# Experts by 64 places, two side by side on TensorE, with unsplit float32 weights

## The chip, the cores and the metric

The kernel runs on 1 core of one Trainium2 chip. The metric is the device time of one execution in microseconds. Three runs of the kernel before took 2030.39, 2038.42 and 2041.88 us; the median is 2038.42 us.

## The reference

Two transformer blocks over 256 tokens of width 1024. The first block is a mixer (Hyena, Fourier and mLSTM branches, merged by gates) and a mixture of experts; the second has four layers of attention and feed-forward. The change is in the mixture of experts, which ends the first block:

```python
g_logits = (t @ moe_rg_w + moe_rg_b)                     # 4 groups, top 1
e_logits = (t @ moe_re_w + moe_re_b).reshape(256, 4, 4)  # 4 experts in each, top 2 of the group chosen
combine  = sum(one_hot(e_idx, 16) * w_sel)               # 256 x 16, two entries a token
hg, hu = t @ moe_w_gate[e], t @ moe_w_up[e]              # 1024 x 256 each, 16 experts
a = silu(hg) * hu * combine
out = sum_e a @ moe_w_down[e]                            # 256 x 1024
x = x + mod_l[5] * out;  then rmsnorm(x, norm_f_w)
```

Every token goes to one group and to two of its four experts. With the inputs that the reference draws, the groups get 58, 53, 86 and 59 tokens, and the fullest expert 53. The weights of one expert are 3 MB of float32, those of all sixteen 50.3 MB.

## The kernel before

Nearly all products are made in three fp32r matmuls: each operand is split into a high and a low part (`split` and `unit`: a copy on ScalarE, line 240, and a subtraction on VectorE, line 242), and `mm3_steps` (lines 254 to 256) multiplies high by high, high by low and low by high. Weights arrive on SyncE's queue in pieces of 512 KB in a ring of `raw` tiles (4 of 4 KB in each partition). Memory is taken by hand from two arenas, one of float32 and one of fp32r words. The order of the instructions on each engine comes from a planner that goes by simulated times, except where `c.after(...)` fixes it; a branch (`tc.If`) is a border that nothing is moved across.

In `moe` the logits are made, then `route` picks group and experts in some forty small VectorE operations. `places` counts by matmuls, for each token, how many of its group come earlier, and loads the largest group's size into a register. `experts` works by groups: a group has 128 places, `oh` holds a 128 x 128 matrix of marks for each half of the tokens and each group, and `gather` (line 1382) multiplies the normed tokens by the marks, which brings the tokens of two groups into their places, already transposed; ScalarE and VectorE scale, shift and split them (lines 1384 to 1386). Then the 16 experts run one after the other over the 128 places of their group. Each has four pieces of gate and up weights (two 256 KB loads, rows of 1 KB, 24 matmuls of 512 columns), SiLU and product (lines 1431, 1433), two transposes (1444) and two pieces of down weights (rows of 4 KB, 12 matmuls of 512 columns). After the fourth expert of a group its sum goes back to the tokens by 8 matmuls with the transposed marks (1417). Five more `raw` tiles and two more pairs serve this stage.

At the end `add_experts` multiplies the sums by the modulation row and adds them to `xs` (lines 1502, 1503). Then a branch (line 1493) would do all experts once more for places 128 and up; it is not taken here. The second block begins in `enter`: VectorE weights the tokens (line 2037), TensorE transposes them (370), they are split, and the first projection starts (264, 265). `mod_row` makes a modulation row from float32 matmuls of 32 columns in four column groups of TensorE (line 684); its calls for row 2 run beside the merging of the branches, those for row 5 fill gaps around the logits. PSUM has 5 buffers `acc` (also used for transposes, `tr`) and 3 buffers `mm`.

Of the kernel before, what the change touches and what calls it, by code (L numbers as in the profile page):

```python
# [29 lines left out]
ARENA = {F32: (22528, 1312), F32R: (29696, 1344)}  # L30
RAW, PAIRS, MM, PROBS, AHEAD = 4, 3, 3, 8, 2
# [45 lines left out]
class Arena:  # L77


    def __init__(self, ap, words, kept):  # L80
        self.ap, self.clock, self.kept, self.words = ap, 0, words - kept, words
        self.free = [(0, words - kept, 0)]
        self.rings, self.groups, self.compact = {}, {}, False

    def alloc(self, n):
        n = -(-n // 16) * 16
        best = None
        for i, (at, _, _) in enumerate(self.free):
            end, age = at, 0
            for j in range(i, len(self.free)):  # L90
                a, b, t = self.free[j]
                if a != end:
                    break
# [12 lines left out]
    def keep(self, n):  # L106

        at = self.kept
        self.kept = at + -(-n // 16) * 16
        assert self.kept <= self.words, self.kept  # L110
        return self.ap[:, at : at + n]
# [4 lines left out]
    def ring(self, group, tag, n, bufs):  # L116
# [9 lines left out]
        return self.ap[:, at : at + n]  # L126

    def release(self, pieces):
        self.free += [(a, b, self.clock) for a, b in pieces]
        merged = []  # L130
        for a, b, t in sorted(self.free):
            if merged and merged[-1][1:] == (a, t):
                a = merged.pop()[0]
# [16 lines left out]
class Core:  # L150


    def __init__(self, tc, I, ctx):
# [7 lines left out]
        for dt, (words, kept) in ARENA.items():  # L161
            t = self.const.tile([P, words], dt, name=f"arena{len(self.arenas)}")
            self.arenas[dt] = Arena(t, words, kept)
        self.raw(), self.split_pair()
# [4 lines left out]
        nc.gpsimd.dma_start(self.ident, I["ident"])  # L169

# [14 lines left out]
    def first_block_done(self):  # L185
        for dt, (_, kept) in ARENA.items():
# [273 lines left out]
def host_constants1():  # L460
# [31 lines left out]
    c["slots"] = f32(np.concatenate([before, np.ones((P, P)), np.tile(s[None], (P, 1))], 1))  # L492
# [16 lines left out]
LATER = (0, 2, 4, 6)  # L509
MORE = (5, 2)  # L510
# [3 lines left out]
FILL = (3, 4, 1)  # L514


class Block1:
# [689 lines left out]
    def mod_row(self, m):  # L1207
# [38 lines left out]
    def route_weights(self):  # L1246
# [4 lines left out]
        self.before, self.ones, self.iota = (const[:, i] for i in range(3))  # L1251
        raw = self.tile((KT, 20), F32, "rwr", 1, "rt")
# [31 lines left out]
    def route(self, pss, r):  # L1284
# [7 lines left out]
        gh = self.gh = self.tile((2, 4), F32, "group", 1, "moe")  # L1292
# [5 lines left out]
        def top(src, oh):  # L1298
# [11 lines left out]
        yield  # L1310
        ex, s = tile(2, 4), tile(2)
        v.tensor_tensor(ex, g, along(mx), ALU.subtract)
        nc.scalar.activation(ex, ex, AF.Exp)
# [7 lines left out]
        m2 = top(eg, h2)  # L1321
        q, d = tile(2), tile(2)
# [10 lines left out]
        v.tensor_tensor(self.comb.rearrange("p t (g j) -> p t g j", g=4),  # L1333
                        h1.rearrange("p t (o j) -> p t o j", o=1).to_broadcast([P, 2, 4, 4]), by, ALU.mult)
        yield

    def places(self):

        c, nc = self.c, self.nc
        ps, sums = c.tr(), c.tr()[:, :4]  # L1340
        gh = self.gh
        mm = nc.tensor.matmul
        mm(ps[:, 0:4], self.before, gh[:, 0], start=True, stop=True)
        mm(ps[:, 4:8], self.before, gh[:, 1], start=True, stop=False)
        mm(ps[:, 4:8], self.ones, gh[:, 0], start=False, stop=True)
        self.pos = self.tile((2, 4), F32, "pos", 1, "moe")
        nc.vector.tensor_copy(self.pos, ps[:, :8].rearrange("p (t g) -> p t g", t=2))
        mm(sums, self.ones, gh[:, 0], start=True, stop=False)
        mm(sums, self.ones, gh[:, 1], start=False, stop=True)
# [6 lines left out]
    def experts(self, xp, first, unit):  # L1356
# [4 lines left out]
        parts = lambda shape, tag, bufs=1: self.parts(shape, tag, bufs, "moe")  # L1361
        pos = self.pos
        if first:
            pos = tile((2, 4), F32, "later")
            nc.vector.tensor_scalar(pos, self.pos, float(-first), None, ALU.add)

        oh, ohT = tile((2, 4, P), F32R, "oh"), tile((4, 2, P), F32R, "ohT")
        for q in range(4):
            for t in range(2):
                nc.vector.tensor_scalar(oh[:, t, q], self.iota, pos[:, t, q : q + 1], self.gh[:, t, q : q + 1], ALU.is_equal, ALU.mult)  # L1370

        def gather(p):
# [818 lines left out]
```

## Time and profile before

| | |
|---|---|
| median of 3 runs | 2038.42 us |
| the profiled execution: time, span | 2037.31 us, 2035.5 us |
| PE, PEld, DVE, ACT busy | 95%, 76%, 66%, 51% |
| granted TensorE clock, mean | 0.973 |
| moved by DMA | 364.61 MB, 179 GB/s |

Times are microseconds from the span's start. The 40 slices of the page are 50.9 us each; the expert stage (459 to 620 us) covers slices 11 and 12 of them, counted from 1, where the DMA engines moved 321 and 323 GB/s, the highest of the page. A float32 matmul stands in the trace as two records, one for each pass; fp32r matmuls as one.

### The profile page before, as it was taken

The numbers are of one execution on the slowest core, as the hardware profiler recorded it, in microseconds if no ns is written. First come the engines' busy times: TensorE is split into PE (matmuls) and PEld (weight loads), VectorE is DVE, ScalarE is ACT, GpSimd is POOL, SyncE is SP. The second block draws the span as 40 slices with busy tenths as digits, with TensorE's granted clock in tenths as the row PEclk, the third lists the DMA queues.
The fourth block names the chain that finished last, engine by engine and source line by source line (L and its number), as shares of the span: only waits on it lengthen the run. The fifth ranks groups of instructions, "written<-read, shape, count | busy, mean of one in ns | idle before, by whom it ended". The sixth has DMA issues, their size and how long they took to land.

```text
span 2035.5 us, 27804 instructions
## 1 busy us (share of the span) xinstructions
PE 1931.8 (95%) x10012; PEld 1546.8 (76%) x10012; DVE 1336.6 (66%) x2324; ACT 1035.3 (51%) x1656; POOL 135.9 (7%) x259
## 2 busy tenths in 40 slices
PE   6998998989998999999999999999999999999997
PEld 2886886867786678887888877887767888767886
DVE  4689887868897775556555466556566555867555
ACT  5555654546774744434655555443563444454442
POOL 2110000000002000002111200000110000300000
PEclk8999998989998899999999999999999999989999
DMA  9546644777995356654543456664554655435662
GB/s 310 162 140 194 183 139 147 236 247 245 321 323 162 116 166 199 186 176 131 170 136 110 147 178 202 191 186 145 156 176 129 201 187 176 155 104 175 188 189 80
DMA packets 272403, 364.61 MB, mean 179 GB/s; under 512 B 17018, under 2 KB 206677, under 8 KB 272256
## 3 DMA queue, kind: packets, MB, share of 16 engines
q1 hardware_dynamic: 264832, 338.38, 52.5%
q0 software_dynamic: 7424, 24.36, 3.8%
q8 instruction: 81, 1.33, 0.3%
q14 instruction: 66, 0.54, 0.1%
HBM read 359.53 MB, written 3.15 MB: 178 GB/s over the span
## 4 chain that ended last, share of the span: by engine, by line
PE 59%; DVE 6%; ACT 2%; DMA 1%; issue 1%; POOL 0%; SPq 0%; DVEq 0%; ACTq 0%; POOLq 0%
PE mm L254 14%; PE mm L255 13%; PE mm L256 13%; PE acc L254 4%; PE acc L256 4%; PE acc L255 4%; PE acc L1752 1%; PE acc L1650 1%; DVE arena L242 1%; PE acc L1929 1%; PE acc L2117 1%; ACT arena L240 1%; DVE arena L2014 1%; PE acc L1749 1%; DMA arena<-in_w_gate_up 1%; PE acc L1925 1%
## 5 line engine op out<-in xcount | busy, mean ns | idle before, releaser
L242 DVE TENSOR_TENSOR arena<-arena,arena 128x1024 fp32r<-128x1024 f32 x597 | 716.9, 1213 | 480.6 <-ACT arena L240 475.8
L240 ACT CAST arena<-arena 128x1024 fp32r<-128x1024 f32 x597 | 614.0, 1039 | 549.4 <-PE mm L256 298.9
L254 PE MATMUL mm<-arena 128*128 128x512 f32 (+1 forms) x1856 | 703.3, 385 | 12.7 <-ACT arena L240 6.8
L255 PE MATMUL mm<-arena 128*128 128x512 f32 (+1 forms) x1856 | 706.0, 381 | 0.3 <-DVE arena L242 0.3
L256 PE MATMUL mm<-arena 128*128 128x512 f32 (+1 forms) x1856 | 698.7, 380 | 3.5 <-DVE arena L1386 1.3
L254 PEld LDWEIGHTS mm<-arena 128*128 128x128 f32 x1856 | 352.9, 191 | 85.8 <-ACT arena L240 8.3
L256 PEld LDWEIGHTS mm<-arena 128*128 128x128 f32 x1856 | 352.3, 191 | 71.2 <-DVE arena L219 4.1
L255 PEld LDWEIGHTS mm<-arena 128*128 128x128 f32 x1856 | 354.0, 191 | 61.5 <-issue 1.8
L254 PE MATMUL acc<-arena 128*128 128x512 f32 (+5 forms) x736 | 235.5, 360 | 7.3 <-ACT arena L218 7.3
L255 PE MATMUL acc<-arena 128*128 128x512 f32 (+5 forms) x736 | 235.4, 351 | 0.5 <-DVE arena L219 0.5
L256 PE MATMUL acc<-arena 128*128 128x512 f32 (+4 forms) x736 | 231.8, 350 | 0.0
L218 ACT CAST arena<-acc 128x512 fp32r<-128x512 f32 (+2 forms) x174 | 92.7, 542 | 179.1 <-PE acc L2117 79.8
L219 DVE TENSOR_TENSOR arena<-acc,arena 128x512 fp32r<-128x512 f32 (+2 forms) x174 | 108.1, 632 | 99.1 <-ACT arena L218 98.7
L254 PEld LDWEIGHTS acc<-arena 128*128 128x128 f32 (+1 forms) x736 | 125.0, 190 | 40.3 <-issue 11.6
L255 PEld LDWEIGHTS acc<-arena 128*128 128x128 f32 (+1 forms) x736 | 125.7, 190 | 21.6 <-issue 1.8
L256 PEld LDWEIGHTS acc<-arena 128*128 128x128 f32 (+1 forms) x736 | 124.7, 190 | 20.5 <-DVE arena L219 1.7
L1685 ACT ACTIVATE arena<-arena,nm 128x128 f32<-128x128 f32 (+2 forms) x128 | 65.9, 517 | 27.1 <-DVE nm L1684 27.1
L768 DVE SCALAR_TENSOR_TENSOR arena<-arena 128x192 f32<-128x192 f32 (+1 forms) x160 | 64.9, 430 | 2.4 <-ACT arena L766 0.9
L1684 DVE CUSTOM_DVE_ANT_0 arena<-acc,arena 128x128 f32<-128x128 f32 (+2 forms) x128 | 53.1, 465 | 13.6 <-PE acc L256 13.6
L370 PE MATMUL acc<-arena 128*128 128x128 f32 x200 | 32.9, 302 | 24.1 <-DVE arena L1020 8.2
L370 PEld LDWEIGHTS acc<-arena 128*128 128x128 f32 x200 | 24.4, 153 | 34.8 <-DVE arena L1020 8.3
L2101 ACT ACTIVATE arena<-mm 128x256 f32<-128x256 f32 x88 | 32.4, 379 | 24.4 <-PE mm L256 11.9
(354 smaller groups left out, 1497.8 us busy)
## 6 DMA issues: line engine op xcount, KB each, us to landing
arena<-in_w_gate_up SPq DMA_DIRECT2D x352, 256.0 KB, 4.0
arena<-in_w_down SPq DMA_DIRECT2D x88, 512.0 KB, 3.6
arena<-in_b_w_qkv SPq DMA_DIRECT2D x144, 256.0 KB, 3.0
arena<-in_w_in SPq DMA_DIRECT2D x56, 512.0 KB, 4.0
arena<-in_ada_w SPq DMA_DIRECT2D x48, 512.0 KB, 5.7
arena<-in_moe_w_gate SPq DMA_DIRECT2D x64, 256.0 KB, 4.6
arena<-in_moe_w_up SPq DMA_DIRECT2D x64, 256.0 KB, 4.9
arena<-in_moe_w_down SPq DMA_DIRECT2D x32, 512.0 KB, 5.3
```

What stands on the lines that cost most here:

```text
L218: self.nc.scalar.copy(h, src)
L219: self.nc.vector.tensor_sub(l, src, h.bitcast(F32))
L240: nc.scalar.copy(h[:, : nk * n], raw[:, : nk * n])
L242: nc.vector.tensor_sub(l[:, : nk * n], raw[:, : nk * n], h[:, : nk * n].bitcast(F32))
L254: yield t.matmul(out, x[0], w[0], start=start, stop=False)
L255: yield t.matmul(out, x[0], w[1], start=False, stop=False)
L256: yield t.matmul(out, x[1], w[0], start=False, stop=stop)
L370: self.nc.tensor.transpose(ps[:, j * P : (j + 1) * P], src[:, j * P : (j + 1) * P], self.ident)
L768: nc.vector.scalar_tensor_tensor(ov[:, rows], x, w, ov[:, rows], ALU.mult, ALU.add)
L1684: nc.vector.tensor_tensor_reduce(pr, s, mask, -0.125, 3e38 if sink is None else sink, ALU.add, ALU.min, nm)
L1685: nc.scalar.activation(pr, pr, AF.Exp, bias=nm, scale=-1.0, accum_out=l)
L2101: nc.scalar.activation(s, ps[:, :256], AF.Silu)
```

## The change

- Each expert has 64 places of its own (`SEATS`), so `marks` are by expert (256 x 16), and `places` counts by expert. The marks are made by two VectorE comparisons of 128 x 1024 instead of eight of 128 x 128.
- Two experts run side by side: one writes PSUM partitions 0 to 63, the other 64 to 127, that is, halves of TensorE's columns. Weights and tokens are plain float32 and are not split: no copy on ScalarE and no subtraction on VectorE for them. Gate and up are matmuls of 256 columns, down of 512.
- Gate and up weights are read as `(p k) n`, four rows of a partition at once: 4 KB rows, 512 KB loads. The gather takes every eighth column of the tokens to match, and scale and shift (`A2e`, `S2e`) are brought into that order through DRAM by four small DMAs on GpSimd's queue.
- 9216 words of the fp32r arena are switched to float32 during the experts: nine further pieces (`MORE`) beside the four `raw` tiles. They are taken in turn.
- The sums: `acc` starts from `xs` (four float32 matmuls with the identity), the modulation row is multiplied in before the marks bring the pair's result back, and 8 matmuls do so for every pair. `add_experts` goes; `enter` reads the sums from PSUM.
- The branch for fuller experts (over 64 tokens; three more passes over all experts) comes inside, behind the second pair's transposes. Behind a pair's SiLU and product come, in this order: the 8 matmuls that bring back the pair before, four transposes (the product and the marks), a part of the next gather, down, and another part of the gather. Two small float32 matmuls a pair turn the token weights into weights of places.
- `mod_row` takes its two PSUM tiles from `mm` instead of `acc`, for row 2 too; the filling is 4, 4 instead of 3, 4, 1 steps.

```diff
+MORE, SEATS, YP, AMID = 9, 64, 2, 1
-FILL = (3, 4, 1)
+FILL = (4, 4)
@@ Core @@
+    def close_switched(self):
+        a = self.arenas[F32R]
+        a.free = [f for f in a.free if f[0] < a.words]
+        self.arenas["switched"] = Arena(self.switched_room(F32, "f"), SWITCHED)
@@ mod_row @@
-            ps, out = c.acc()[:, :256], c.acc()
+            ps, out = c.mm()[:, :256], c.mm()
@@ route @@
+        v.tensor_tensor(both, h1, h2, ALU.add)
+        v.tensor_tensor(self.marks.rearrange("p t (g j) -> p t g j", g=4), spread(both), by, ALU.mult)
@@ experts @@
+        def mark():
+            seats = self.iota[:, :SEATS].rearrange("p (o s) -> p o s", o=1).to_broadcast([P, 16, SEATS])
+            for t in range(2):
+                at = pos[:, t].rearrange("p (e o) -> p e o", o=1).to_broadcast([P, 16, SEATS])
+                nc.vector.tensor_tensor(oh[:, t], seats, at, ALU.is_equal)
+        def gather_two(h, g, k):
+            ps = c.mm().rearrange("p (k s) -> p k s", k=2)
+            for j in range(2):
+                cols = slice(k + j, None, KT)
+                for i in range(4):
+                    mm(ps[:, j], xp[i // 2][i % 2][:, cols], marks(i // 2, 4 * g, 4), start=i == 0, stop=i == 3)
+                nc.scalar.activation(h[:, k + j], ps[:, j], AF.Identity, bias=self.S2e[:, k + j], scale=self.A2e[:, k + j])
+        def scatter(p, ohT, y):
+            yp = self.parts((D,), "y", YP, "moe")
+            for n in range(2):
+                sl = slice(512 * n, 512 * n + 512)
+                f = tile((512,), F32, "yf", 2)
+                nc.vector.tensor_tensor(f, y[n], self.rows[5][:, sl], ALU.mult)
+                c.split(*(a[:, sl] for a in yp), f)
+            yield
+            for t in range(2):
+                for n in range(2):
+                    for i in range(2):
+                        mm(acc[t][n], ohT[:, t], yp[i][:, 512 * n : 512 * n + 512], start=False, stop=first == 0 and p == 7 and i == 1)
+            yield
+        for p in range(8):
+            if p % 2 == 0 and p < 6:
+                later = gather(p // 2 + 1)
+            hq = [h[:, :, p % 2 * P + 64 * e : p % 2 * P + 64 * e + 64] for e in range(2)]
+            ps = c.acc()
+            for k in range(0, KT, 4):
+                for i, name in enumerate(("moe_w_gate", "moe_w_up")):
+                    us = [load(I[name][0, 2 * p + e].rearrange("(p k) n -> p k n", p=P)[:, k : k + 4]) for e in range(2)]
+                    for j in range(4):
+                        for e in range(2):
+                            mm(ps[64 * e : 64 * e + 64, 256 * i : 256 * i + 256], hq[e][:, k + j], us[e][:, j], start=i + k + j == 0, stop=i + k + j == KT)
...
+            nc.scalar.activation(s, ps[:, :256], AF.Silu)
+            nc.vector.scalar_tensor_tensor(a, ps[:, 256:], weight[:, p : p + 1], s, ALU.mult, ALU.mult)
+            next(late, None)
...
+            if p == AMID and amid is not None:
+                with self.tc.If(amid > SEATS):
+                    for n in range(SEATS, 256, SEATS):
+                        self.experts(xp, acc, n, raw)
+                    mark()
+                    for k in range(0, KT // 2, 2):
+                        gather_two(following, 1, k)
+            following = next(later, None)
+            y = [c.mm(), c.mm()]
+            for kk in range(2):
+                wd = [load(I["moe_w_down"][0, 2 * p + e, kk * P : (kk + 1) * P].rearrange("p (o n) -> p o n", o=1)) for e in range(2)]
+                for n in range(2):
+                    for e in range(2):
+                        mm(y[n][64 * e : 64 * e + 64], aT[:, kk, 64 * e : 64 * e + 64], wd[e][:, 0, 512 * n : 512 * n + 512], start=kk == 0, stop=kk == 1)
+            late = scatter(p, ohT, y)
+            next(late)
+            following = next(later, None)
@@ moe @@
+        c.close_switched()
+        acc = [[c.acc() for n in range(2)] for t in range(2)]
+        for t in range(2):
+            for n in range(2):
+                with c.after(c.last(PE)):
+                    nc.tensor.matmul(acc[t][n], c.ident, xs[t][:, 512 * n : 512 * n + 512], start=True, stop=False)
-        self.add_experts(self.experts(xp, 0, unit), xs)
-        with self.tc.If(most > P):
-            self.add_experts(self.experts(xp, P, own_unit), xs)
+        self.experts(xp, acc, 0, lambda: next(rooms), most)
@@ enter @@
-                nc.vector.tensor_tensor(zs[t][:, sl], xs[t][:, sl], nf[:, sl], ALU.mult)
+                nc.vector.tensor_tensor(zs[t][:, sl], ps, nf[:, sl], ALU.mult)
```

## Rows read from the trace of the kernel before

**Rows 1.** The page: busy time of the engines, and the chain's shares by engine.
```profile
PE 1931.8 (95%) x10012; PEld 1546.8 (76%) x10012; DVE 1336.6 (66%) x2324; ACT 1035.3 (51%) x1656; POOL 135.9 (7%) x259
PE 59%; DVE 6%; ACT 2%; DMA 1%; issue 1%; POOL 0%; SPq 0%; DVEq 0%; ACTq 0%; POOLq 0%
```

**Rows 2.** Windows: length, busy PE, PEld, DVE, ACT, POOL; clock, DMA share, GB/s.
```profile
459.00:619.60 160.60, 154.10 (x688) 123.16 (x687) 136.46 (x151) 116.86 (x149) 0.00 (x0) 0.99 0.86 288
540.00:600.00 60.00, 60.00 (x268) 48.60 (x268) 54.78 (x58) 46.96 (x59) 0.00 (x0) 1.00 1.02 346
570.00:580.00 10.00, 10.00 (x46) 8.10 (x45) 9.37 (x11) 7.90 (x9) 0.00 (x0) 1.00 1.07 372
619.60:629.10 9.50, 1.82 (x9) 1.60 (x9) 6.78 (x13) 3.52 (x4) 2.10 (x4) 0.62 0.11 33
326.00:374.00 48.00, 47.43 (x280) 37.50 (x279) 39.20 (x59) 19.47 (x30) 3.88 (x8) 1.00 0.66 224
```

**Rows 3.** Groups by line, 459 to 619.6: busy us, mean ns, idle before.
```profile
L242 DVE TENSOR_TENSOR arena<-arena,arena 128x1024 fp32r<-128x1024 f32 x92 | 110.4, 1223 | 17.5 <-ACT arena L240 15.3 <-DMA arena<-in_moe_w_up 0.6 <-DMA arena<-in_moe_w_down 0.3
L254 PE MATMUL mm<-arena 128*128 128x512 f32 x160 | 64.6, 404 | 0.0
```

**Rows 4.** Chain of waits by time, 640 us: start, us, what (start to start).
```profile
640.00 0.24 PE mm L254
640.23 0.23 PE mm L255
```

**Rows 5.** Timeline, end of the stage: start, us, engine, line, tiles, [idle before, releaser].
```profile
617.23 2.36 PE L1417 MATMUL acc<-arena 128*128 128x512 f32 x8
618.93 1.29 DVE L1502 TENSOR_TENSOR arena<-acc,arena 128x512 f32<-128x512 f32 x2 [0.32 <-PE acc L1417]
626.53 2.50 DVE L2037 TENSOR_TENSOR arena<-arena 128x512 f32<-128x512 f32 x4 [2.72 <-DVEq L1493]
627.27 1.97 PE L370 MATMUL acc<-arena 128*128 128x128 f32 x8 [7.68 <-DVE arena L2037]
629.07 0.80 PE L264 MATMUL mm<-arena 128*128 128x512 f32 x1
```

**Rows 6.** Line 1493, the branch: count, ns min/median/max, first to last start.
```profile
L1493 PEldq COMPARE_BRANCH  x1: 3599/3599/3599, 618.7 to 618.7; - x1
L1493 SPq COMPARE_BRANCH  x1: 50/50/50, 614.9 to 614.9; - x1
L1493 SPq EVENT_SEMAPHORE  x8: 17/17/17, 619.2 to 619.7; - x8
```

**Rows 7.** Timeline of PE: float32 in column groups, and what follows.
```profile
428.15 1.50 PE L684 MATMUL acc<-arena 128*32 128x256 f32 x24
429.59 0.33 PE L370 MATMUL acc<-arena 128*128 128x128 f32 x1
...
1080.64 1.09 PE L1929 MATMUL acc<-arena 128*64 128x128 f32 x16
1081.67 0.50 PE L254 MATMUL mm<-arena 128*128 128x512 f32 x1
```

**Rows 8.** Timeline of PE: gather, transposes, small float32 matmuls, first expert.
```profile
529.57 0.63 PE L1382 MATMUL mm<-arena 128*128 128x256 f32 x4
530.03 0.38 PE L1444 MATMUL mm<-arena 128*128 128x128 f32 x2
...
456.95 1.92 PE L1399 MATMUL acc<-arena,arena 128*128 128x4 f32 x16 [0.18 <-DVE arena L1333]
458.73 0.48 PE L254 MATMUL mm<-arena 128*128 128x512 f32 x1
```

**Rows 9.** Lines 1382, 1384 and 1370 alone: ns min/median/max, first to last.
```profile
L1382 PEld LDWEIGHTS mm<-arena x64: 186/188/338, 450.4 to 532.9; 128*128 128x128 f32 x64
L1384 ACT ACTIVATE arena<-mm,arena x16: 557/564/567, 451.8 to 533.4; 128x256 fp32r<-128x256 f32 x16
L1370 DVE TENSOR_SCALAR arena<-arena x8: 337/340/345, 449.3 to 451.3; 128x128 fp32r<-128x128 f32 x8
```

**Rows 10.** Timeline: routing's small operation, and the first gather.
```profile
447.00 0.17 DVE L1305 TENSOR_TENSOR arena<-arena,r 128x8 f32<-128x8 f32 x1
...
450.38 2.27 PE L1382 MATMUL mm<-arena 128*128 128x256 f32 x12 [0.85 <-DVE arena L1370]
```

More of the change, by code (lines that the diff above doesn't have):

```diff
@@ L30 @@
 ARENA = {F32: (22528, 1312), F32R: (29696, 1344)}
+SWITCHED = 9216
 RAW, PAIRS, MM, PROBS, AHEAD = 4, 3, 3, 8, 2
@@ L91, in alloc @@
                 a, b, t = self.free[j]
-                if a != end:
+                if a != end or i < j and a == self.words:
                     break
@@ L1354, in places, with experts @@
         return nc.values_load(most_i[0:1, 0:1], min_val=0, max_val=256)
-    def experts(self, xp, first, unit):
+    def experts(self, xp, acc, first, raw, amid=None):
         c, nc, I = self.c, self.nc, self.I
         tile = lambda shape, dt, tag, bufs=1: self.tile(shape, dt, tag, bufs, "moe")
-        parts = lambda shape, tag, bufs=1: self.parts(shape, tag, bufs, "moe")
+        mm = nc.tensor.matmul
         pos = self.pos
         if first:
-            pos = tile((2, 4), F32, "later")
+            pos = tile((2, 16), F32, "later")
@@ L1389, in marks_T @@
-        def marks_T(q):
-            ps = c.mm()
-            for t in range(2):
-                nc.tensor.transpose(ps[:, t * P : (t + 1) * P], oh[:, t, q].bitcast(F32), c.ident)
-            nc.scalar.copy(ohT[:, q].rearrange("p t s -> p (t s)"), ps[:, : 2 * P])
-        *_, h = gather(0)
-        wp = c.tr()
-        for q in range(4):
-            for t in range(2):
-                nc.tensor.matmul(wp[:, 4 * q : 4 * q + 4], oh[:, t, q].bitcast(F32), self.comb[:, t, 4 * q : 4 * q + 4], start=t == 0, stop=t == 1)
@@ new lines, in experts @@
+        late, later = iter(()), iter(())
+        for p in range(8):
+            if p % 2 == 0 and p:
+                h = following
+            if p % 2 == 0 and p < 6:
[8 more added lines that the diff above has]
+                            mm(ps[64 * e : 64 * e + 64, 256 * i : 256 * i + 256], hq[e][:, k + j], us[e][:, j], start=i + k + j == 0, stop=i + k + j == KT)
+            wp = c.mm()[:, :2]
+            for t in range(2):
+                mm(wp, marks(t, 2 * p, 2).bitcast(F32), self.comb[:, t, 2 * p : 2 * p + 2], start=t == 0, stop=t == 1)
+            for e in range(2):
+                rows = slice(64 * e, 64 * e + 64)
+                nc.scalar.copy(weight[rows, p : p + 1], wp[rows, e : e + 1])
@@ L1451, in moe @@
+            next(late)
+            following = next(later, None)
+        next(late)
     def moe(self, xs, fill):
         c, nc = self.c, self.nc
+        c.close_switched()
         def filler(n):
@@ L1571, in run @@
                 self.dump(f"mix{t}", xs[t])
-            self.moe(xs, self.mod_row(5))
-            for t in range(2):
-                self.dump(f"moe{t}", xs[t])
+            sums = self.moe(xs, self.mod_row(5))
             drop("moe", "mrow5")
-        return xs
+        return xs, sums
 def rope_tables(c):
```

193 lines of the change are left out of this document (86 added, 107 removed).

## The prediction

> **What bounds the kernel now.** The page comes first. TensorE is busy 95% of the span and holds 59% of the chain; VectorE follows with 66% and 6% [rows 1]. So a change pays where it takes TensorE's time away or closes a gap of it, unless the weights then arrive too slowly. The windows of the expert stage come next. From 459.0 to 619.6, 160.6 us, TensorE is busy 154.1 at a clock of 0.99, and the DMA engines move 288 GB/s; from 540 to 600 TensorE has no gap at all, while the DMA share stands at 1.02 and 346 GB/s [rows 2]. Two limits therefore lie close together here, and the change touches both. The groups by line say what TensorE does: 160 matmuls of 512 columns on line 254, as many on 255 and 256, and 32 on each of the three lines for down, 576 in all; VectorE spends 110.4 us on the low parts of weights [rows 3]. In a dense stretch a matmul follows the other every 0.23 us [rows 4], so that 576 make 133 us of the stage's 160.6. Last comes its end in the timeline: the last sum is done at 619.6, VectorE adds it to the tokens, passes the branch, and only at 629.07 does the second block's first projection start [rows 5].
>
> I compare the time between two events that both kernels have: the first expert matmul, at 458.73 [rows 8], and that first projection, at 629.07 [rows 5]: 170.3 us.
>
> **Part by part, TensorE.** Two experts in two halves of the columns, in float32, two passes each. The trace has this form: line 1929, 64 columns wide, 16 records from 1080.64 to the next matmul at 1081.67, 1.03 us. If the halves ran one after the other, these would be 16 steps of 128 columns; line 684 makes six steps of four groups with 256 columns in 1.44 us (428.15 to 429.59) [rows 7]. With x for a step of 128 columns, 2x for 256 and s for entering and leaving the form, 8x + s = 1.03 and 12x + s = 1.44, so x = 0.10 and s = 0.2. Eight steps, not sixteen, fit: the halves do run together. I take 0.215 for 256 columns (bounds 0.205 and 0.24, that is 1.44/6) and 0.43 for 512.
>
> Of a pair: gate and up are 8 slices of the depth by 2 names by 2 passes, 32 steps of 256, 6.9 us; down is 2 by 2 by 2, 8 steps of 512, 3.4 us. Eight pairs make 82.6 us. Bringing the results back is 8 matmuls for every pair instead of every four experts: 64 by 0.231 = 14.8 us. The gathers of groups 1 to 3 stay on this path: 96 matmuls by 0.115 (four from 529.57 to 530.03 [rows 8]) = 11.0. Transposes, four a pair, 32 by 0.12 (0.19 at most, a pair of them 0.38 [rows 8]) = 3.8. The small float32 matmuls are 4 records a pair by 0.11 (16 from 456.95 to 458.73 [rows 8]) = 3.6. Entering and leaving the halves twice a pair by 0.2 = 3.4. Sum 119.2 us, where 154 were busy.
>
> Waits on this path: the first pair has nothing to fill the time of SiLU and product, 1.0; the last two pairs have no gather between transposes and down, 0.8 each; behind the last down three evacuations of some 0.65 (as line 1502 [rows 5]) and their signals, 2.2. Sum 4.8. In the other pairs the 8 matmuls of the pair before (1.86) cover SiLU and product, and a part of the gather (0.9) covers the copies.
>
> The branch. TensorE's own jump took 3.6 us at 618.7, SyncE's 4.2 (614.9 to 619.2) [rows 6]. It now falls between full engines, and what hid it (the end of the stage) is gone: 3.6, and 1.0 more because the clock had fallen to 0.62 in the gap around the old one [rows 2]. Behind SyncE's branch stand all loads from the second pair's down weights on. Before it twenty pieces are issued, so TensorE has work for one and a half pairs, about 20 us, while the queue stands; I cost that at nothing. If the eight waits that followed SyncE's branch [rows 6] now hold it until the loads in flight have landed, up to 8 us.
>
> Its sum: 119.2 + 4.8 + 4.6 = 128.6 us from the first expert matmul to the last sum; before it was 160.9 (458.73 to 617.23 + 2.36).
>
> **The splits** go: 92 subtractions of 1.2 us [rows 3] and as many copies. VectorE is left with about 4 us a pair, ScalarE with 4.5 (two gather activations of 0.56 [rows 9] in each part included); neither is late. What is late next is TensorE itself, and close to it the weights.
>
> **The weights.** 96 pieces of 0.524 MB. Thirteen fit; I take them as there when the first pair starts, as their room comes free when the merging ends. The other 83 are 43.5 MB: at 372 GB/s, the best ten microseconds before [rows 2], 117 us, which with 4 us for the last to land and 6 for what follows it is 127, just inside 128.6. At 346 it is 126 + 10 = 136. Rows of 4 KB alone do not occur in a row of the trace; I take 372 as the value, as the stretch with 346 was bound by TensorE. The Trainium skill (DMA: Bandwidth & Descriptors, Specifications) gives 358 GB/s as one core's share of the memory; the 372 here is above it, and the measurement decides. By the page's figure the estimate would be 121.5 + 10 = 131.5, 3 us more.
>
> **Ahead of the stage.** Counting now needs both choices, about 14 small operations more at 0.2 us each in the chain (0.17 busy [rows 10]), +2.8. Against it VectorE is free of weight splits that stood between these operations, -3; two comparisons of 1.2 us replace eight of 0.34 [rows 9], 0; the four added matmuls with the identity (8 passes of 0.43, 3.4 us) lie beside the routing. The first gather, at 450.38 [rows 10], takes 8 activations of 0.56, 4.5 us. I leave 458.7 as the start, within 5 us on either side.
>
> **Behind the stage.** `add_experts` and the branch go from the chain: instead of 9.5 us from the last sum to the projection [rows 5], I reckon 4.5: one weighting, 0.65, straight from PSUM, two transposes with their splits. Four of five `acc` buffers are still held there, so transposes go one by one: the second half of the tokens pays 3 more later on (0 to 4). And row 2's `mod_row` takes `mm` buffers from the merging in a stretch where TensorE is busy 47.4 of 48 us [rows 2]: 2 (0 to 5).
>
> Sum: 128.6 + 4.5 = 133.1 against 170.3, -37; +5 for the last two; so -32 from the profiled execution's 2037.3 (span 2035.5 and 1.8 around it): 2005. This execution lies 1.1 below the median of the runs, so I call it 2005 to 2006 and give 2005.
>
> **Rivals.**
> - *The weights set the end.* 346 GB/s or less, or SyncE held behind the branch: +8 to +15, 2013 to 2020. For it: DMA share 1.02 already at 346 [rows 2]. Against: 372 was reached with shorter rows.
> - *The gather's strided columns.* Its stationary operand, now every eighth float32, is loaded more slowly than in 188 ns [rows 9]. The slowest load of that line, at the lower clock, took 338 [rows 9]; a step of 0.23 instead of 0.115 for 128 matmuls is +15, 2020. The sign turns where a gather matmul takes 0.25 us more (32/128), a step of 0.37; at 0.48 it is +47, 2052, slower than before. For it: all 128 gather matmuls stand on TensorE's path. Against: nothing in the trace reads with this step, but a load lies beside the matmul before it. The Trainium skill speaks for it (SBUF — State Buffer, Door 1: The DMA port swizzle): memory lines are 16 bytes, and every access to a new line pays; a step of 32 bytes meets a new line each time. No row here shows such a load.
> - *It doesn't do what it says*: an expert with over 64 tokens takes the branch, three more passes of at least 117 us, near 2400. The fullest has 53; next to nothing.
>
> **How the numbers follow.** Forecast 0.62 (its own range 1996 to 2012); weights 0.17; gather at about double 0.12; gather slow enough to be slower than before, with the branch taken, 0.05; nearly no change, by several half-sized losses, 0.04. Runs of this kernel can't tell less than about 0.5% (10 us) from no change. Faster: 0.62 + 0.17 + 0.12 = 0.91, and 0.01 of the fourth case's edge, 0.92; same 0.03; slower 0.05. Range: below, the start 5 us early, no loss at the end and behind (-5) and a dearer merging spared (-2), 1993; above, weights and a doubled gather in part together, 2026.
>
> **What would show it.** After: no line-242 work in the stage; the last sum some 128 us after the first expert matmul; steps of 0.215 with both halves starting together; gather steps of 0.115; at the second pair one gap of about 4 us on TensorE; the DMA near 340 to 375 GB/s. Wrong if TensorE has gaps that end with a landing weight in most pairs, if gather steps are 0.2 and more, if the clock falls in the stage for longer than at the branch, or if the stretch around 326 to 374 grows by more than 5 us.

## The result, and the profile after

The changed kernel is slower. Its median is 2049.2 us (2047.6 to 2056.9, 12 runs) beside 2033.6 us of the kernel before on the same chips (12 runs): a ratio of 1.0073, 95% interval 1.0055 to 1.0090, some 15 us. The forecast was 2005. The profiled execution took 2048.9 us, its span 2047.1. Line numbers below are those of the changed kernel unless another is named.

The page of the changed kernel, its first part and the chain's shares by engine, beside [rows 1]:

```profile
span 2047.1 us, 27688 instructions
PE 1943.5 (95%) x10188; PEld 1515.4 (74%) x10188; DVE 1212.8 (59%) x2192; ACT 948.9 (46%) x1587; POOL 138.6 (7%) x263
PE 65%; DVE 6%; ACT 2%; DMA 1%; issue 1%; POOL 0%; DVEq 0%; SPq 0%; ACTq 0%; POOLq 0%
```

The splits are gone (VectorE 124 us less than before), yet TensorE is busy 12 us longer. Where the time went is seen by comparing events that both kernels have. The first token transposes for the logits start at 418.3 instead of 409.0: 9.3 us are lost before the experts begin. The first expert matmul stands at 469.6 (before 458.7 [rows 8]), the second block's first projection at 641.2 (before 629.1 [rows 5]): 171.6 us where 133.1 were forecast and 170.3 stood before. From there to the end of the span the two kernels take the same time to within 1 us (1406.4 before, 1406.0 now).

Windows of the changed kernel; columns as in [rows 2]:

```profile
200.00:255.00 55.00, 43.51 (x304) 37.25 (x293) 35.27 (x79) 27.46 (x56) 3.49 (x9) 0.78 0.74 172
469.60:639.50 169.90, 154.52 (x866) 90.56 (x866) 28.36 (x48) 38.09 (x86) 3.23 (x6) 0.98 0.78 280
```

In the stage the DMA engines move 280 GB/s, less than the 372 that the kernel before reached for ten microseconds [rows 2], and in the list of TensorE's waits none in the stage ends with a landing weight, so the weights don't set the end. VectorE is busy 28 of 170 us. What is left is TensorE, 154.5 us of it, where the forecast had 119. The first window belongs to a stretch that the prediction didn't look at. There the kernel before reads so:

```profile
200.00:255.00 55.00, 48.77 (x381) 43.59 (x378) 46.70 (x103) 34.16 (x69) 0.77 (x8) 0.94 0.66 192
```

**Ahead of the stage.** GpSimd's timeline of the changed kernel (start, duration), and the DMA issues from 200 to 260 us (KB each, median us to landing):

```profile
201.90 0.91 POOL L1285 DMA_DIRECT2D mod<-arena  x1 [5.84 <-DVE arena L739]
215.18 0.56 POOL L1287 DMA_DIRECT2D arena<-mod  x1 [12.26 <-DMA mod<-arena]
228.59 0.91 POOL L1285 DMA_DIRECT2D mod<-arena  x1 [12.74 <-DVE arena L1234]
239.50 0.55 POOL L1287 DMA_DIRECT2D arena<-mod  x1 [8.58 <-DMA mod<-arena]
```
```profile
arena<-in_w_in SPq DMA_DIRECT2D x15, 512.0 KB, 6.0
arena<-in_ada_w SPq DMA_DIRECT2D x4, 512.0 KB, 11.2
mod<-arena POOLq DMA_DIRECT2D x2, 4.0 KB, 13.0
```

The same view of the kernel before:

```profile
arena<-in_w_in SPq DMA_DIRECT2D x16, 512.0 KB, 3.8
arena<-in_ada_w SPq DMA_DIRECT2D x4, 512.0 KB, 5.3
```

Line 1285 is the turn of scale and shift: 1024 elements of 4 bytes, each to a place of its own in DRAM. The first of these transfers of 4 KB lands after 13.0 us (the trace has no landing of the second; what reads it starts 10.9 us behind it), and the pieces of `in_ada_w` issued from 200 to 260 land after 11.2 instead of 5.3 (medians of four). The rate of all DMA in that stretch, in slices of 1.5 us, GB/s, in the changed kernel and in the kernel before:

```profile
GB/s 80 241 364 356 363 52 3 58 30 32 110 379 337 290 182 252 317 240 282 287 36 16 23 38 23 23 16 204 328 290 294 225 254 19 5 30 314 5 176 184
GB/s 185 349 325 401 142 194 379 139 223 264 326 300 291 287 293 269 201 271 82 226 124 198 152 206 143 5 119 231 156 205 0 0 0 0 5 101 249 161 188 0
```

While a 4-byte write is under way, the changed kernel moves 3 to 58 GB/s (207.5 to 215.0 and 230.0 to 240.5), although weights are asked for: a piece issued at 202.4 lands at 215.7. TensorE waits for these pieces, in part by way of their splits on ScalarE.

**The gather.** All instructions of its line (duration ns: min/median/max), in the changed kernel; [rows 9] has 186/188/338 for the loads before:

```profile
L1428 PEld LDWEIGHTS mm<-arena x128: 312/338/344, 462.1 to 603.5; 128*128 128x128 f32 x128
L1428 PE MATMUL mm<-arena x128: 283/407/603, 462.2 to 603.7; 128*128 128x256 f32 x128
```

**A steady pair** (from the transposes of one pair's product to those of the next), 526.03 to 547.65, 21.6 us, from TensorE's timeline of the changed kernel:

```profile
526.03 0.44 PE L1488 MATMUL mm<-arena 128*128 128x128 f32 x2 [1.03 <-DVE arena L1484]
526.30 0.38 PE L1490 MATMUL mm<-arena,arena 128*128 128x128 f32 x2
526.44 1.23 PE L1428 MATMUL mm<-arena 128*128 128x256 f32 x4
527.60 3.65 PE L1508 MATMUL mm<-switched_f,arena 128*64 128x512 f32 x12
531.17 1.24 PE L1428 MATMUL mm<-arena 128*128 128x256 f32 x4
532.34 0.64 PE L1508 MATMUL mm<-switched_f,arena 128*64 128x512 f32 x1
...
532.82 1.45 PE L1508 MATMUL mm<-switched_f,arena 128*64 128x512 f32 x3
534.21 1.25 PE L1428 MATMUL mm<-arena 128*128 128x256 f32 x4
...
537.59 0.74 PE L1458 MATMUL acc<-arena 128*128 128x512 f32 x2
538.16 1.01 PE L1428 MATMUL mm<-arena 128*128 128x256 f32 x4
539.01 0.62 PE L1458 MATMUL acc<-arena 128*128 128x512 f32 x2
539.56 0.65 PE L1474 MATMUL acc<-arena 128*64 128x256 f32 x2
540.14 1.20 PE L1458 MATMUL acc<-arena 128*128 128x512 f32 x4
...
547.65 0.44 PE L1488 MATMUL mm<-arena 128*128 128x128 f32 x2 [1.00 <-DVE arena L1484]
```

This is not the order of the text. The 16 records of down (line 1508) are cut up: eight run two at a time, four alone behind them, and after a part of the gather the last four alone again: 12 steps of 0.43, where 8 were reckoned. The sums of the pair before (1458) stand in the middle of gate and up, so that nothing is left to fill the wait for SiLU and product, 1.03 us at the head of every pair.

**The branch**, line 1496, in SyncE's and TensorE's timelines and in SyncE's waits (us in total, times, longest):

```profile
476.73 2.38 SPq L1444 DMA_DIRECT2D switched_f<-in_moe_w_up  x2
500.19 2.37 SPq L1444 DMA_DIRECT2D switched_f<-in_moe_w_down  x3
```
```profile
498.03 0.38 PE L1490 MATMUL mm<-arena,arena 128*128 128x128 f32 x2
501.79 1.33 PE L1428 MATMUL mm<-arena 128*128 128x256 f32 x4 [3.38 <-ACTq L1496]
503.83 1.33 PE L1428 MATMUL mm<-arena 128*128 128x256 f32 x4 [0.72 <-ACT arena L1429]
505.09 3.68 PE L1508 MATMUL mm<-switched_f,arena 128*64 128x512 f32 x4
```
```profile
SPq L1444 <- PEq L1496: 12.0, 1, 12.0
```

SyncE is at the branch from 479.2 on. Its eight waits there end at 488.0, when the last load in flight has landed; its first load behind them waits 12.0 us more and goes out at 500.2, once TensorE has passed the branch too. For 21 us no weight is asked for, and those for the down matmuls of this very pair are among the missing. Behind TensorE's gap of 3.38 us four down matmuls take 3.68 us, as the clock has fallen (0.59 from 505 to 510).

### The profile page after: what moved, and what is told of

It reads as the page before. It is cut to its first block, busy times and chain, and to the rows that moved or that the text cites. A ratio compares the mean times of both kernels' runs of the same rounds, so it can differ in the third digit from the quotient of the medians.

```text
span 2047.1 us, 27688 instructions
## 1 busy us (share of the span) xinstructions
PE 1943.5 (95%) x10188; PEld 1515.4 (74%) x10188; DVE 1212.8 (59%) x2192; ACT 948.9 (46%) x1587; POOL 138.6 (7%) x263
## 4 chain that ended last, share of the span: by engine, by line
PE 65%; DVE 6%; ACT 2%; DMA 1%; issue 1%; POOL 0%; DVEq 0%; SPq 0%; ACTq 0%; POOLq 0%
PE mm L285 14%; PE mm L286 13%; PE mm L287 13%; PE acc L285 4%; PE acc L287 4%; PE acc L286 4%; PE acc L1474 2%; PE mm L1508 2%; PE mm L1428 1%; PE acc L1704 1%; PE acc L2171 1%; PE acc L1983 1%; PE acc L1806 1%; DVE arena L2068 1%; DMA arena<-in_w_gate_up 1%; DVE switched_r L273 1%
## 5 line engine op out<-in xcount | busy, mean ns | idle before, releaser
L271 ACT CAST arena<-arena 128x1024 fp32r<-128x1024 f32 (+1 forms) x449 | 461.2, 1034 | 488.7 <-PE mm L287 249.4
L285 PE MATMUL mm<-arena 128*128 128x512 f32 (+1 forms) x1458 | 549.4, 384 | 15.3 <-ACT arena L271 8.0
L287 PE MATMUL mm<-arena 128*128 128x512 f32 (+1 forms) x1490 | 557.5, 378 | 1.8 <-DVE arena L765 1.8
L273 DVE TENSOR_TENSOR arena<-arena,arena 128x1024 fp32r<-128x1024 f32 (+1 forms) x302 | 361.4, 1201 | 298.9 <-ACT arena L271 297.5
L286 PE MATMUL mm<-arena 128*128 128x512 f32 (+1 forms) x930 | 343.2, 369 | 0.3 <-DVE arena L273 0.3
L285 PEld LDWEIGHTS mm<-arena 128*128 128x128 f32 x1458 | 279.4, 193 | 74.0 <-ACT arena L271 9.7
L287 PEld LDWEIGHTS mm<-arena 128*128 128x128 f32 x1490 | 285.6, 192 | 56.0 <-DVE arena L765 2.2
L286 PE MATMUL mm<-switched_r,arena 128*128 128x512 f32 x718 | 286.0, 398 | 0.0
L273 DVE TENSOR_TENSOR switched_r<-arena,arena 128x1024 fp32r<-128x1024 f32 x147 | 179.7, 1223 | 142.4 <-ACT arena L271 142.2
L286 PEld LDWEIGHTS mm<-arena 128*128 128x128 f32 x930 | 182.0, 196 | 27.0 <-issue 2.2
L285 PE MATMUL acc<-arena 128*128 128x512 f32 (+3 forms) x532 | 178.4, 369 | 2.7 <-ACT arena L249 2.7
L286 PEld LDWEIGHTS mm<-switched_r,arena 128*128 128x128 f32 x718 | 135.1, 188 | 28.8
L287 PE MATMUL acc<-arena 128*128 128x512 f32 (+1 forms) x404 | 154.3, 387 | 0.0
L286 PE MATMUL acc<-arena 128*128 128x512 f32 (+1 forms) x392 | 150.3, 385 | 0.0
L285 PEld LDWEIGHTS acc<-arena 128*128 128x128 f32 (+1 forms) x532 | 90.9, 188 | 27.6 <-issue 7.8
L285 PE MATMUL mm<-switched_r,arena 128*128 128x512 f32 x190 | 75.9, 400 | 0.0
```

The lines of the kernel that those rows point to most:

```text
L271: nc.scalar.copy(h[:, : nk * n], raw[:, : nk * n])
L273: nc.vector.tensor_sub(l[:, : nk * n], raw[:, : nk * n], h[:, : nk * n].bitcast(F32))
L285: yield t.matmul(out, x[0], w[0], start=start, stop=False)
L286: yield t.matmul(out, x[0], w[1], start=False, stop=False)
L287: yield t.matmul(out, x[1], w[0], start=False, stop=stop)
```

## The experiments

Times are medians; the ratio is to the kernel before on the same chip (medians 2033.2 to 2034.3), with its 95% interval. "Stage" is the profiled execution's time from the first expert matmul to the second block's first projection, "pair" its steady pair. A ratio is known to some 0.16% (3 us) either way, so a difference between two kernels to 4 or 5 us; the differences below are of medians. What lies behind that projection also differs from one execution to the next: 1405.7 to 1418.9 us in the profiles of the change and runs 1, 2, 3, 5, 6 and 7, though TensorE's order there is the same but for a few rows.

| kernel | us | ratio | stage | pair |
|---|---|---|---|---|
| the change | 2049.2 | 1.0073 [1.0055, 1.0090] | 171.6 | 21.6 |
| 1 turn by TensorE | 2035.2 | 1.0020 [1.0004, 1.0036] | 171.3 | 21.6 |
| 2 plain gather | 2035.8 | 1.0022 [1.0009, 1.0034] | 161.1 | 19.9 |
| 3 no branch | 2035.4 | 1.0009 [0.9991, 1.0027] | 157.2 | 18.4 to 22.3 |
| 4 written order | 2053.8 | 1.0111 [1.0082, 1.0140] | 165.8 | 19.5 |
| 5 = 1 + 2 | 2026.3 | 0.9958 [0.9941, 0.9974] | 161.4 | 19.8 |
| 6 = 5 + order | 2014.0 | 0.9904 [0.9888, 0.9921] | 144.7 | 15.7 |
| 7 = 6, no branch | 2001.7 | 0.9832 [0.9812, 0.9853] | 131.5 | 15.7 |
| **8 = 6, branch first** | **2001.9** | **0.9840 [0.9824, 0.9856]** | 136.5 | 15.7 |
| 9 = 8, rows of 1 KB | 2007.4 | 0.9862 [0.9846, 0.9878] | 141.4 | 15.7 to 18.0 |
| 10 = 8, planner's order | 2028.2 | 0.9970 [0.9958, 0.9982] | 161.4 | 20.0 |
| 11 = 8, activations between | 2013.6 | 0.9891 [0.9874, 0.9907] | 147.4 | 17.6 |
| 12 = 8, the 4-byte turn back | 2014.8 | 0.9904 [0.9888, 0.9921] | 134.6 | 15.7 |

**1. The turn.**

```diff
-            nc.gpsimd.dma_start(d.rearrange("(k p) -> p k", p=P), m...)
+            nc.tensor.transpose(ps[:KT, :P], m..., c.ident)
+            nc.scalar.copy(rows[:KT], ps[:KT, :P])
+            nc.gpsimd.dma_start(d.rearrange("(k p) -> k p", p=P), rows[:KT])
```

> One edit to the changed kernel: scale and shift are turned by a TensorE transpose each and written to DRAM as 8 rows of 512 bytes, in place of 1024 elements of 4 bytes each. Theory A: the two writes of 4-byte elements (201.9 to 214.9 and 228.6 to about 241 us in the trace of the changed kernel) hold the DMA engines, so that weight pieces issued beside them land after 11 to 14 us instead of 4; the changed kernel's lag of 9.3 us at its first token transposes (418.27 against 408.99) comes from them alone. Then this kernel is 8 to 10 us faster than the changed one, near 2040, and the window 200 to 255 has TensorE busy as before (48.8 of 55 us, 43.5 in the changed kernel). Rival: the lag comes from mod_row in other PSUM tiles or from the rearranged memory; then the time stays within 2 us of 2049.

It is 13.9 us faster than the changed kernel, and the stage itself doesn't move (171.3). The window that had lost TensorE's work has it back:

```profile
200.00:255.00 55.00, 49.03 (x381) 44.09 (x382) 47.34 (x108) 34.83 (x72) 1.51 (x10) 0.94 0.67 192
```

Theory A stands for the turn as a whole; its price is 13.9 by the medians and 10.8 by the ratios, beside the 9.3 read from one execution. One thing more has changed: the two writes, now of rows of 512 bytes, land after 3.4 and 1.8 us, but the planner has also moved them to 374.2 and 386.5, out of this window. What the same rows would cost at 202, or the 4-byte writes at 374, no run shows.

**2. The gather's columns.**

```diff
-                cols = slice(k + j, None, KT)
+                cols = slice((k + j) * P, (k + j + 1) * P)
-                nc.scalar.activation(h, xs[t], AF.Copy, ...)
+                nc.scalar.activation(by(h), xs[t].rearrange("p (q k) -> p k q", k=KT), AF.Copy, ...)
```

(VectorE's low part in the same way; `by` views `h` as 8 by 128.)

> One edit: the normed tokens are stored in the order in which the gather wants them (ScalarE and VectorE read them with a step of eight when they make the two parts), so that the 128 gather matmuls load 128 neighbouring columns instead of every eighth. Theory A: the step of 0.245 us of these matmuls in the changed kernel comes from the strided load; it falls to 0.115 to 0.13, 128 times, so 15 to 17 us less, 2032 to 2034, of which 4 at the first gather and 12 in the stage. Rival: the stage is bound by something else (weights, or the two column halves), and the time on the gather comes back as a wait: less than 5 us, 2044 or more. What could be lost: two reads on each of ScalarE and VectorE with a step, under 1 us together.

13.4 us less (10.4 by the ratios), with the stage's order on TensorE the same but for one row, and the loads are short again (the same view as above):

```profile
L1428 PEld LDWEIGHTS mm<-arena x128: 186/189/333, 458.4 to 588.1; 128*128 128x128 f32 x128
L1428 PE MATMUL mm<-arena x128: 274/282/582, 458.4 to 588.2; 128*128 128x256 f32 x128
```

The step from one matmul to the next falls from 0.245 to 0.12. Theory A stands in the step; it had 15 to 17 us.

**3. No branch.** The `If` and its body are left out.

> One edit: the branch behind the second pair is left out (and with it the passes for experts with over 64 tokens, which these inputs don't have). Theory A: the branch costs what the second of the pairs with a branch takes more than a steady pair, 28.2 - 21.65 = 6.6 us: 3.4 of gap on TensorE, the slower clock behind it, and weights that stand behind SyncE's branch (no load is issued between 478.4 and 500.2). So 2042 to 2043. Rival: the queue's pause costs nothing further, since the loads in front of it last, and the gap alone goes: 3.5 to 4, 2045. A second rival: without this border the planner mixes the matmuls of the two halves with others still more, and the time stays or grows.

13.8 us less, twice what theory A had. In the stage 14.4 us go: the second pair falls from 28.2 to 20.1 us, and the other 6 come from the other pairs, most of them shorter (18.4 to 20.3, one 22.3). The planner orders otherwise without the border: of the 128 records of down 11 run alone instead of 36. So this run changes two things, the branch and the order, and the second rival came out the other way.

**4. The written order alone.**

```diff
+        def mm(*a, **o):
+            with c.after(c.last(PE)):
+                nc.tensor.matmul(*a, **o)
```

> One edit: every TensorE instruction of the expert stage is held behind the one before it in the program's text, so that the planner can't put matmuls of the gather or of the sums between those of the two halves, nor the sums of the pair before ahead of SiLU. Theory A: the changed kernel's steady pair of 21.65 us holds 1.55 us of down matmuls that run in one half alone (12 steps of 0.43 where 8 do), 1.0 of the same in gate and up, 1.4 of waiting for SiLU and product that the sums (2.25) no longer cover, and 0.4 in the sums: 4.3 a pair, some 7 pairs, 25 to 30 us less, 2020 to 2025. Rival: halves alone are a result of weights that land one after the other, not of the order; then the order as written waits for the weights instead, and the time is 2045 or more.

Theory A falls in the total: 2053.8, 4.6 us more than the change (the two intervals overlap). In the stage it is half right. The pair shrinks from 21.6 to 19.5, and down takes 3.65 us for all 16 records. But TensorE now waits inside each part of the gather, twice a pair (timeline of this kernel):

```profile
551.48 1.22 PE L1408 MATMUL mm<-arena 128*128 128x256 f32 x4
553.35 1.23 PE L1408 MATMUL mm<-arena 128*128 128x256 f32 x4 [0.66 <-ACT arena L1437]
```

Both groups of four write one PSUM tile, and the second waits until ScalarE has read the first; the planner's order had hidden that. The first gather, held too, has the same waits and a granted clock of 0.53 from 460 to 473 (the first expert matmul at 473.0), and what lies behind the stage took 5 us more, no more than it differs elsewhere. So the rival, that halves alone come from landing weights, isn't borne out either.

**5 to 8. Together, then the order, then the branch.** Six adds to five the order of 4 for the loop alone (the first gather stays free) and puts both activations behind both groups of four:

```diff
             for j in range(2):
                 for i in range(4):
                     mm(ps[:, j], ...)
-                nc.scalar.activation(h[:, k + j], ps[:, j], ...)
+            for j in range(2):
+                nc.scalar.activation(h[:, k + j], ps[:, j], ...)
```

Eight takes the branch out of the loop and puts it ahead, in `moe`; the sums start from `xs` and all passes add to them, so the order of the passes is free:

```diff
+        with self.tc.If(most > SEATS):
+            for n in range(SEATS, 256, SEATS):
+                self.experts(xp, acc, n, lambda: next(rooms))
         self.experts(xp, acc, 0, lambda: next(rooms), most)
```

> The edits of the first two experiments together: scale and shift turned by TensorE, and the tokens stored in the gather's order. Theory A: the two costs lie in different places (200 to 255 us, and the gathers from 440 us on) and add up: 13.9 + 13.4 less than the changed kernel, 2022. Rival: both act on the start of the stage and share a part, since the gather of the first group waits there for the same weights and the same clock; then 2027 to 2031.

> The kernel of the experiment before (turn and gather), with TensorE's instructions in the loop over pairs held in the written order, and both groups of four gather matmuls put ahead of their two activations. From the run with the written order alone: gate and up 7.2, down 3.65, sums 2.0, transposes 0.6, weights of places 0.5 and, at 0.12 a matmul, gather 1.9 us: pairs of 15.9, where 19.9 stood in the run with the plain gather. Theory A: order and gather were the two losses inside the pair; five pairs by 4 and the last two by 2.5 are some 22 less than the turn and gather alone: 2000. Rival: the weights (12 pieces of 1.25 us make 15.0, and SyncE's pause at the branch has to be made up) now set the pair: 17 to 18 us, 2008 to 2012, with waits of TensorE that end with landing weights.

> As the kernel with turn, gather and written order, without the branch (and so without the passes for experts with over 64 tokens). Theory A: with pairs of about 16 us the weights run close behind, so the pause of 22 us in SyncE's issues is paid nearly whole: 8 to 12 us less than with the branch. Rival: only the jump goes, 3.5 to 5.

> As the kernel with turn, gather and written order, with the branch moved ahead of the first pair: the passes for fuller experts come first, and no weight is loaded before the branch is passed. Theory A: the branch's pause lies where TensorE waits for the routing anyway, but the thirteen pieces that were there at the first pair now start some 10 us later: first pair 5 us later, then as without the branch: 3 to 6 us less than with the branch behind the second pair. Rival: the stage turns into one bound by weights from its start (96 pieces by 1.25 us = 120 us, from the branch on) and is not faster than with the branch inside.

Five came out at 2026.3, between its two theories. By the medians the gather is worth 8.9 beside the turn and 13.4 alone, by the ratios 12.6 and 10.4: whether the two share a part isn't shown. Six gave 12.3 more and stands above both its theories. Its pairs are 15.7, as theory A had it (15.9), but the second takes 28.7, and there the rival was right on SyncE's pause. From TensorE's timeline of run six:

```profile
485.72 7.40 PE L1413 MATMUL mm<-switched_f,arena 128*64 128x512 f32 x16 [2.12 <-ACT arena L1443]
```

The four down pieces of this pair land at 485.6, 486.9, 489.9 and 491.1, and the matmuls follow them: 2.1 us of waiting for the first (the row names ScalarE, but the piece lands 0.1 us before the matmul starts), then 7.40 us in place of 3.65, at a granted clock of 0.50 from 486 to 490. Three more waits, 2.3 us together, end with landing gate and up weights. With the gap of 3.4 at the branch that is 11.6 of the 13.0 us by which the pair is longer. Seven, without the branch, is 12.3 faster and its stage takes 131.5 us. Eight is as fast as seven with the branch in it: better than both theories, and it beats the kernel before by 1.6%. In the profiles seven is 11.4 us ahead of eight at the projection (581.7 against 593.0) and loses 8 of them behind it; its clock reads 0.83 there from 1450 to 1500, that of eight 0.97. A steady pair of eight, in TensorE's timeline:

```profile
533.77 0.38 PE L1417 MATMUL mm<-arena 128*128 128x128 f32 x2
533.98 0.38 PE L1417 MATMUL mm<-arena,arena 128*128 128x128 f32 x2
534.12 1.20 PE L1413 MATMUL mm<-arena 128*128 128x256 f32 x8
535.25 3.65 PE L1413 MATMUL mm<-switched_f,arena 128*64 128x512 f32 x16
538.83 1.22 PE L1413 MATMUL mm<-arena 128*128 128x256 f32 x8
...
547.04 0.61 PE L1413 MATMUL mm<-arena,arena 128*128 128x2 f32 x4
547.51 2.10 PE L1413 MATMUL acc<-arena 128*128 128x512 f32 x8
549.44 0.38 PE L1417 MATMUL mm<-arena 128*128 128x128 f32 x2
```

Eight gather matmuls take 1.2 us where four did, all 16 records of down 3.65, and the sums (547.51) stand where SiLU and product are waited for: no wait is left.

**9. Rows of 1 KB.** As eight, with nothing turned and nothing permuted:

```diff
-...rearrange("(p k) n -> p k n", p=P)[:, k : k + 4]
+...rearrange("(k p) n -> p k n", p=P)[:, k : k + 4]
```

> As the kernel with the branch first, but gate and up weights read with four rows of 1 KB in each partition, so that tokens, scale and shift keep the order they have: no turn and no permuted storing at all. Theory A: the rows matter. In the run with the branch first TensorE is busy without a gap and the DMA engines move 403 to 421 GB/s from 470 to 540 us; with rows of 1 KB the best stretch of the kernel before had 372. Two thirds of the bytes are gate and up, so the 48 MB take some 8% longer on these, about 6 to 9 us more: 2008 to 2011. Rival: the rate hangs on the number of pieces in flight, not on the rows; then 2002, less up to 1 us for what is left out.

5.5 us slower than eight by the medians, just under theory A, 4.5 by the ratios; the two intervals overlap, so the totals alone don't settle it. The same window in eight and then in nine:

```profile
470.00:540.00 70.00, 70.00 (x486) 44.08 (x484) 14.35 (x23) 20.55 (x50) 0.00 (x0) 0.98 1.02 414
```
```profile
470.00:540.00 70.00, 70.00 (x495) 43.45 (x493) 15.29 (x24) 20.24 (x48) 0.00 (x0) 0.99 1.07 387
```

A steady pair takes 12 pieces of 0.524 MB in 15.67 us, 401 GB/s. At 387 the weights fall behind, and late in the stage TensorE waits for landing ones (pairs of 17.1 and 18.0). The 4 KB rows can earn this only now that TensorE uses weights so fast; in the changed kernel, at 280 GB/s, no wait of TensorE's ended with one.

**10 to 12. Each mended part undone in eight.** Ten leaves out the order (and the moved activations), eleven puts the activations back between, twelve writes 4-byte elements again.

> As the kernel with the branch first, but the planner's order on TensorE again (and the gather's activations between its groups of four). Theory A: the order is worth what it was worth with the branch inside (2026.3 to 2014.0): 12, so 2014. Rival: the planner went wrong because of the branch inside, as its pairs of 18.4 to 22.2 us in the run without the branch and its 21.65 with it suggest; then 5 to 7 of these, 2007 to 2009.

> As the kernel with the branch first, but each activation of the gather directly behind its four matmuls again, in the written order. Theory A: the second four wait for the first activation, as both use one PSUM tile (0.66 us, twice a pair, in the run with the written order alone): six pairs by 1.3, 8 us more, 2010. Rival: the weights run at 403 to 421 GB/s anyway and take up a part: 2 to 4 us more.

> As the kernel with the branch first, but scale and shift turned by the 4-byte writes again. Theory A: these writes cost 13 to 14 us wherever the stage stands, as between the changed kernel and the run that took them away alone (2049.2 and 2035.2): 2015. Rival: the profile's reading, 9.3 us at the first token transposes, was the price, and the other 4 to 5 came from another planned order: 2011.

Ten is 26.2 us slower than eight; both its theories had half of that or less. Its pairs of 20.0 begin with the old wait for SiLU and product. Eleven costs 11.7: 2.0 a pair in place of the 1.3 of theory A, and against its rival. So of ten's 26 the order alone is worth 14.5 and the place of the activations, once the order is held, 11.7; the small gain of run 4 inside the stage (5.8) fits with that. Twelve costs 12.8 (13.0 by the ratios), as its theory A had it, with the writes back at 200.4 and 226.8, though its profiled execution starts the experts only 5.9 later (462.4 against 456.5). That execution was the fastest of its four (2008.1 to 2016.9, where eight's lie within 2001.1 to 2005.4): in this kernel the price seems to differ from run to run. What it hangs on stays open.

## Why the prediction was wrong

By the sum's own parts the miss of 44 us is made of four. Undone one behind the other they give 47: the turn 13.9, the gather 8.9 beside it, order and activations 12.3, the branch 12.1 (by the ratios 10.8, 12.6, 11.0 and 13.0). For the branch the forecast held 4.6 already; what is left, 2001.9, and these 4.6 make 2006.5, 1.5 above the forecast. That they meet so closely is partly luck: run seven starts the experts 8.6 us before the 458.7 of the forecast, its stage is 3 us over, and behind it its profile takes 12.5 us more than the kernel before.

- *A term that was missing.* "Ahead of the stage" counted VectorE's operations, the added matmuls and the first gather's activations. The four small DMAs ahead of the change got no price, although two of them write elements of 4 bytes (the line taken out in run one). The step "I leave 458.7 as the start, within 5 us" fell with it. Apart from the page's totals [rows 1] no row of the prediction lies between 200 and 255 us: it looked only where the text of the kernel has the change, and the planner had put `route_weights` far ahead of that. The Trainium skill (DMA: Bandwidth & Descriptors, Rules for kernel authors) says that a last dimension that isn't contiguous becomes one descriptor an element; the 13.0 us for 4 KB fit that, but the trace lists no such descriptors.
- *The gather.* "96 matmuls by 0.115" failed; the rival with 0.23 was right in mechanism and nearly in size (0.245). The argument against it, that a load lies beside the matmul before it, doesn't save the step: with loads of 338 ns it is 0.245 us, with 189 ns 0.12. The Trainium skill (SBUF — State Buffer, Door 1: The DMA port swizzle) says that memory lines are of 16 bytes and each access to a new one pays, which spoke for the rival; 338 and 189 ns for the same load with and without the step of 32 bytes agree. The rival deserved more than 0.12.
- *The order.* "The halves do run together" held: steps of 0.216, both halves starting within 7 ns. That "the 8 matmuls of the pair before (1.86) cover SiLU and product" did not, since it was read from the text, while a planner orders this kernel. In the planner's order a pair is 19.8 with the plain gather (run five); in the written one, with the activations moved, 15.7, where the prediction's terms give 15.3. The written order alone would not have done it: a part of the gather waits inside for its first activation, a wait that the sum put at nothing and that is worth 2.0 a pair in run eleven.
- *The branch.* TensorE's own part was as reckoned (3.4 against 3.6). "I cost that at nothing", for SyncE, was the failed step: its eight waits hold it until the loads in flight have landed, as the prediction allowed for, and its first load then holds it longer still, until TensorE is past the branch. The price is 12.1 to 12.3 in place of 4.6 once the pairs are short; the upper bound that the prediction gave for a held SyncE, 8 more, was about the size.
- *The weights* were priced too dear: 414 GB/s for 70 us in run eight, where 372 was taken. Of that rival (0.17) only the second half came, SyncE held behind the branch; in the changed kernel no wait of TensorE's in the stage ended with a landing weight, while in run six those behind the branch did.
- *Behind the stage and row 2.* 1.7 us from the end of the last sum to the projection (4.5 forecast), and no growth from `mod_row`: in run one the kernel stands 7.4 us ahead of the kernel before at the matmul that sums the router's shift (385.1 against 392.6), with `mod_row` as changed. Both were costed too high, 5 us together. The transposes that go one by one cost about what was forecast (2 us some 40 us behind the projection, 3 forecast); further on that is made up.

So the arithmetic of the new form was near (stage 133.1 forecast, of which 4.6 for the branch; 131.5 in run seven, which has none, 136.5 in run eight), and what lies around it wasn't: what feeds it, in which order it is issued, and what stops the queue.

## What to carry to other kernels

Price each DMA of a change by its elements and not by its bytes, at the place where the planner will put it, and look there for what shares the engines. Where a planner orders the engines, cover and adjacency that a text promises have to be held, or else counted as not there. Ask of a branch when the first load behind it can go out, and put it where no load is held up by it.

## What had not been expected of the hardware

- A 4 KB write in 4-byte elements took 13.0 us to land (10.8 to 13.0 in the five kernels that have it at this place), and while it was under way the core's DMA fell to 3 to 58 GB/s; the same 4 KB in rows of 512 bytes, at another place, took 3.4 and 1.8 us.
- Loads of a stationary operand whose columns are 32 bytes apart took 338 ns instead of 189, and matmuls of 256 columns then followed each other in 0.245 us instead of 0.12.
- One core's loads from DRAM ran at 403 to 421 GB/s in every stretch of ten microseconds from 460 to 540 in run eight, rows of 4 KB; with rows of 1 KB at 387.
